# Edge aggregation on one core: dense count matrices in PSUM in place of a one-hot gather and scatter per destination tile

## The chip, the cores and the metric

The kernel runs on one core of a Trainium2 chip. The metric is the device time of one execution in microseconds (us), as the median of several runs. The core has five engines with instruction streams of their own: TensorE (PE; its weight loads are listed as PEld, its sequencer as PEq and PEldq), VectorE (DVE), ScalarE (ACT), GpSimd (POOL) and SyncE (SP), and 16 DMA engines behind queues that the engines issue to. SBUF is the on-chip memory of 128 partitions, PSUM the accumulator memory that PE writes.

## The reference

```python
N, E, D = 4096, 262144, 256
# nodes (N, D) fp32; edges_src, edges_dst (E,) int64 in [0, N); w_msg, w_self (D, D) fp32
self_out = nodes @ w_self
msg = nodes[edges_src] @ w_msg
agg = zeros((N, D)); np.add.at(agg, edges_dst, msg)
return self_out + agg
```

Each of 262,144 edges adds the transformed row of its source node to the row of its destination node. Sources and destinations are drawn at random.

## The kernel before, in words

*Keys and sort.* Each edge becomes one fp32 number that holds an integer: the tile of its destination (dst >> 7, 32 tiles of 128 nodes) in the high bits, then its source (12 bits), then dst & 127. The edges come in two halves, each with a load of 1 MB on SP's queue and on ACT's, and seven DVE instructions per half build the keys (L138 to L146). `_run_sort` sorts all 2^18 keys with a bitonic network of 18 stages. A stage is a series of DVE passes of min and max (`cpass`, L455 and around); from the eleventh stage on, each stage also transposes the 128 x 2048 array by 16 PE transposes into the layout B (L391) and 16 back (L399), whose PSUM results ACT and DVE copy out in turn. At the end the sorted keys lie as XA (rank along the free dimension) and as XB, in which a column holds 128 consecutive keys, one per partition.

*TT.* While DVE sorts, PE and ACT build TT: 256 blocks of 128 consecutive node rows in bf16, each 16 rows further than the one before, made by products with shift matrices (473 matmuls and 256 ACT copies).

*Windows.* A count over every 128th key tells for each of the 32 tiles in which column of XB its edges begin. DVE loads 31 of these numbers into a register, one by one (L190), and copies 72 columns each (L192) into a window. 18 wide passes (L202 to L210, twice) split the keys into source and destination.

*Tile loop.* For each tile, 72 chunks of 128 edges. `prep` makes the first source of each chunk, rounded down to 16, and the number of the block of TT that covers it (`bidx`, memory for PE's registers). `slabs` makes one-hot matrices for 12 chunks at a time: Sslab (128 edges x 12 chunks x 128 destinations, L261) and Eslab (the same with sources relative to the block, L268), 6 + 6 instructions on DVE per tile, the chunk being the middle dimension and the compared column the innermost. `chunkloop` runs on PE: two products Eslab^T x Sslab (L301) give a 128 x 128 count matrix of source by destination per chunk, ACT copies the pair to bf16 (L309), and a second product multiplies it with the block of TT (L316, 256 columns), adding up in agg_ps. The block's address is a register that PE's sequencer has loaded, eight at a time (`load_reg_group`, TENSOR_LOAD at L291), and turned into an address by an instruction that the order lists as ISA and the trace as FUSED_REGOPS. `tail` transposes the sum, multiplies it with w_msg and the tile's nodes with w_self, and stores 128 rows.

The Tile framework places waits by the names of tiles; within an engine the instructions run in the order of the program (a scheduler may move them, and the rows in the section on the change are in the final order).

Of the kernel before, what the change touches and what calls it, by code (L numbers as in the profile page):

```python
# [9 lines left out]
P = 128  # L10
FP32 = mybir.dt.float32
# [5 lines left out]
AX = mybir.AxisListType  # L17

CAP = 72
SLAB = 12  # L20
TT_GRAN = 16
LAG = 4
# [7 lines left out]
def kernel(  # L30
# [9 lines left out]
    nc = tc.nc  # L40
# [29 lines left out]
    iota_i = const.tile([P, P], I32, name="iota_i")  # L70
    nc.gpsimd.iota(iota_i[:], pattern=[[1, P]], base=0, channel_multiplier=0)
    iota_row = const.tile([P, P], BF16, name="iota_row")
    nc.vector.tensor_copy(out=iota_row[:], in_=iota_i[:])
    ones_col = const.tile([P, 1], FP32, name="ones_col")
    nc.vector.memset(ones_col[:], 1.0)
    e00 = const.tile([P, P], FP32, name="e00")
    nc.gpsimd.memset(e00[:], 0.0)
    nc.gpsimd.memset(e00[0:1, :], 1.0)
    shz = const.tile([P, P], BF16, name="shz")
    nc.gpsimd.memset(shz[:], 0.0)  # L80
    shA = const.tile([P, NB8, P], BF16, name="shA")
    shB = const.tile([P, NB8, P], BF16, name="shB")
    for s in range(NB8):
        nc.gpsimd.affine_select(
            out=shA[:, s, :],
            in_=shz[:],
            compare_op=ALU.not_equal,
            fill=1.0,
            base=-TT_GRAN * s,
            pattern=[[-1, P]],  # L90
            channel_multiplier=1,
        )
        nc.gpsimd.affine_select(
            out=shB[:, s, :],
            in_=shz[:],
            compare_op=ALU.not_equal,
            fill=1.0,
            base=-TT_GRAN * s + P,
            pattern=[[-1, P]],
            channel_multiplier=1,  # L100
        )

    wcat = finp.tile([P, 4, D], BF16, name="wcat")
    nc.gpsimd.dma_start(wcat[:, 0:2, :], w_self.rearrange("(k p) f -> p k f", p=P))
    nc.gpsimd.dma_start(wcat[:, 2:4, :], w_msg.rearrange("(k p) f -> p k f", p=P))

    nodes_bf_dram = dram.tile([N, D], BF16, name="nodes_bf_dram")

    wbuf0 = wp.tile([P, T, WIN], FP32, name="wbuf0")
    wbuf1 = wp.tile([P, T, WIN], FP32, name="wbuf1")  # L110
    k16 = wp.tile([P, G16], FP32, name="k16")
    Mcmp = wp.tile([P, T, G16], FP32, name="Mcmp")
    Srow = wp.tile([P, T], FP32, name="Srow")
# [8 lines left out]
    XB = [sortp.tile([P, XBW], FP32, name=f"XB{i}") for i in range(2)]  # L122

    HC = NCOL // 2
    ekey = XA[1][:].bitcast(I32)[:, 0:HC]
    etmp = XA[1][:].bitcast(I32)[:, HC:2 * HC]
    for h in range(2):
        d64 = XB[0][:, 0:NCOL].bitcast(I64)
        s64 = XB[1][:, 0:NCOL].bitcast(I64)
# [8 lines left out]
        nc.vector.tensor_single_scalar(out=ekey, in_=dlo, scalar=7, op=ALU.logical_shift_right)  # L138
        nc.vector.tensor_single_scalar(out=ekey, in_=ekey, scalar=19, op=ALU.logical_shift_left)
        nc.vector.tensor_single_scalar(out=etmp, in_=slo, scalar=7, op=ALU.logical_shift_left)  # L140
        nc.vector.tensor_tensor(out=ekey, in0=ekey, in1=etmp, op=ALU.bitwise_or)
        nc.vector.tensor_single_scalar(out=etmp, in_=dlo, scalar=127, op=ALU.bitwise_and)
        nc.vector.tensor_tensor(out=ekey, in0=ekey, in1=etmp, op=ALU.bitwise_or)
        nc.vector.tensor_copy(out=XA[0][:, h * HC:(h + 1) * HC], in_=ekey)
    for i in range(2):
        nc.gpsimd.memset(XB[i][:, NCOL:XBW], SENT_KEY)  # L146

    stgn = tc.alloc_tile_pool(name="stage_n", bufs=1)
    nodes_bf = stgn.tile([P, N // P, D], BF16, name="nodes_bf")
    nc.gpsimd.dma_start(nodes_bf[:], nodes.rearrange("(b p) f -> p b f", p=P))  # L150
    nc.sync.dma_start(nodes_bf_dram.rearrange("(b p) f -> p b f", p=P), nodes_bf[:])
    psum_tt = tc.alloc_tile_pool(name="psum_tt", bufs=1, space=bass.MemoryType.PSUM)
    for k in range(NBLK):
        j0, s = divmod(k, NB8)
        ttps = psum_tt.tile([P, D], FP32, name="tt_ps", tag="ttps", bufs=2)
        two = (s != 0) and (j0 < (N // P) - 1)
        nc.tensor.matmul(  # L157
            out=ttps[:], lhsT=shA[:, s, :], rhs=nodes_bf[:, j0, :], start=True, stop=not two
        )
        if two:  # L160
            nc.tensor.matmul(  # L161
                out=ttps[:], lhsT=shB[:, s, :], rhs=nodes_bf[:, j0 + 1, :],
                start=False, stop=True,
            )
        nc.scalar.copy(out=TT[:, k, :], in_=ttps[:])  # L165
    psum_tt.release()
    stgn.release()

    psum_sort = tc.alloc_tile_pool(name="psum_sort", bufs=1, space=bass.MemoryType.PSUM)
    _run_sort(nc, psum_sort, XA, XB, ident, NCOL, NSTAGE, JBITS, G16)  # L170

    nc.vector.tensor_copy(out=k16[:], in_=XA[0][:, 0::P])
    for t in range(T):
        nc.vector.tensor_scalar(
            out=Mcmp[:, t, :], in0=k16[:], scalar1=float(t << 19), scalar2=None, op0=ALU.is_lt
        )
    nc.vector.tensor_reduce(out=Srow[:], in_=Mcmp[:], axis=AX.X, op=ALU.add)
    c0_ps = psum_sort.tile([1, T], FP32, name="c0_ps")
    nc.tensor.matmul(out=c0_ps[:], lhsT=ones_col[:], rhs=Srow[:], start=True, stop=True)
    nc.vector.tensor_scalar(  # L180
        out=startf[:], in0=c0_ps[:], scalar1=-1.0, scalar2=0.0, op0=ALU.add, op1=ALU.max
    )
    nc.vector.tensor_copy(out=starti[:], in_=startf[:])
    psum_sort.release()

    for t in range(T):
        if t == 0:
            src_view = XB[0][:, 0:WIN]
        else:
            c0 = nc.vector.value_load(starti[0:1, t:t + 1], min_val=0, max_val=NCOL - 1)  # L190
            src_view = XB[0][:, bass.ds(c0, WIN)]
        nc.vector.tensor_copy(out=wbuf0[:, t, :], in_=src_view)  # L192

    TW = T * WIN
    HT = TW // 2
    w0f = wbuf0[:].rearrange("p t w -> p (t w)")
    w1f = wbuf1[:].rearrange("p t w -> p (t w)")
    for h in range(2):
        hs = slice(h * HT, (h + 1) * HT)
        tmp1 = XA[1][:].bitcast(I32)[:, 0:HT]  # L200
        tmp2 = XB[1][:, 0:NCOL].bitcast(I32)[:, 0:HT]
        nc.vector.tensor_copy(out=tmp1, in_=w0f[:, hs])  # L202
        nc.vector.tensor_single_scalar(out=tmp2, in_=tmp1, scalar=7, op=ALU.logical_shift_right)
        nc.vector.tensor_single_scalar(out=tmp2, in_=tmp2, scalar=4095, op=ALU.bitwise_and)
        nc.vector.tensor_copy(out=w1f[:, hs], in_=tmp2)
        nc.vector.tensor_single_scalar(out=tmp2, in_=tmp1, scalar=19, op=ALU.logical_shift_right)
        nc.vector.tensor_single_scalar(out=tmp2, in_=tmp2, scalar=7, op=ALU.logical_shift_left)
        nc.vector.tensor_single_scalar(out=tmp1, in_=tmp1, scalar=127, op=ALU.bitwise_and)
        nc.vector.tensor_tensor(out=tmp2, in0=tmp2, in1=tmp1, op=ALU.bitwise_or)
        nc.vector.tensor_copy(out=w0f[:, hs], in_=tmp2)  # L210
    sortp.release()
    wdst = wbuf0
    wsrcf = wbuf1

    psum = ctx.enter_context(tc.tile_pool(name="psum", bufs=1, space=bass.MemoryType.PSUM))
    bidxp = ctx.enter_context(tc.tile_pool(name="bidxp", bufs=1))
    bidx_all = bidxp.tile([1, T * WIN], I32, name="bidx_all")
    tp_pool = ctx.enter_context(tc.tile_pool(name="tilework", bufs=2))
    oh_pool = ctx.enter_context(tc.tile_pool(name="onehot", bufs=4))
# [271 lines left out]
```

## Time and profile before

| | us |
|---|---|
| median of 3 runs | 1254.68 (1254.49 to 1255.6) |
| span of the profiled execution | 1253.1 |
| keys | 0 to 27.2 |
| first ten sort stages, with TT built beside them | 27.2 to 166.0 |
| other sort stages, with transposes | 166.0 to 520.1 |
| windows | 520.1 to 567.6 |
| tile loop | 567.6 to 1243.8 |
| tail after the last slab | 1243.8 to 1253.1 |

The stages were cut by the times of the first and last instruction of the lines above. The page says of a span how much of it each engine was busy; a busy engine is one on which an instruction of its data path runs. Loads of registers, address arithmetic, waits and branches are not in that share, and have rows of their own under the names of the sequencers. The row of a group of instructions gives the line, engine, operation, output and inputs, their shapes and count, and after the bar the total busy time in us and the mean of one in ns, then the idle time of the engine just before them. The row of a stage gives, after its limits and length, the busy time (and count) of PE, PEld, DVE, ACT and POOL in it, then the granted clock of PE as a share of full speed, the busy share of the DMA engines and GB/s.

### The profile page before, as it was taken

To read this page: it belongs to the slowest core of one execution; us is meant where nothing else is said; L and a number is where in the kernel's file an instruction comes from. 1 tells how busy PE (TensorE), PEld (TensorE's weight loads), DVE (VectorE), ACT (ScalarE), POOL (GpSimd) and SP (SyncE) were. 2 spreads that over 40 slices of the span, in tenths; PEclk is the share of its full clock that TensorE was granted. 3 is DMA by queue.
4 is the path that set the end of the run, shared out by engine and by line. 5 is a ranking of instruction groups with operands and counts; after the bars stand their busy time and mean duration, and the time that the engine had idled before them with its cause. 6 is when DMAs were issued, how large, how long until landed. Compare 5 with 4: busy or idle time off the path is not lost.

```text
span 1253.1 us, 18139 instructions
## 1 busy us (share of the span) xinstructions
PE 674.5 (54%) x5611; PEld 500.7 (40%) x5611; DVE 1171.3 (93%) x1207; ACT 550.6 (44%) x1641; POOL 8.7 (1%) x31
## 2 busy tenths in 40 slices
PE   0777221212121121105777777777777777787777
PEld 0444110111010010004556655655665656565655
DVE  5999989899989989859999999999999999999997
ACT  0777211101010010104656565666666666665665
POOL 2000000000000000000000000000000000000000
PEclk9999665555565555557999899989899989999999
DMA  9100000000000000000000000000000000000000
GB/s 226 51 1 1 0 1 0 0 0 1 0 0 0 0 0 1 0 0 7 12 8 14 8 14 8 14 8 14 8 15 8 14 8 14 8 14 8 14 8 9
DMA packets 24279, 16.11 MB, mean 13 GB/s; under 512 B 10880, under 2 KB 23680, under 8 KB 23680
## 3 DMA queue, kind: packets, MB, share of 16 engines
q1 hardware_dynamic: 16944, 8.40, 2.3%
q0 software_dynamic: 4656, 2.36, 1.4%
q10 hardware_dynamic: 2592, 4.20, 0.9%
q8 instruction: 54, 0.88, 0.3%
q14 instruction: 33, 0.27, 0.1%
HBM read 8.91 MB, written 6.29 MB: 12 GB/s over the span
## 4 chain that ended last, share of the span: by engine, by line
DVE 90%; PE 5%; issue 2%; DMA 1%; DVEq 1%; ACT 0%; ACTq 0%
DVE Eslab L268 25%; DVE Sslab L261 25%; DVE XA_151 L430 5%; DVE XA_150 L430 5%; DVE XA_151 L431 5%; DVE XA_150 L431 5%; DVE XB_152 L430 3%; DVE XB_153 L430 3%; PE tp_sw L391 3%; DVE XB_153 L431 3%; DVE XB_152 L431 3%; DMA XB_152<-in_edges_dst_dram 1%; DVEq L190 1%; DVE base_i L228 1%; DVE wbuf_136 L192 0%
## 5 line engine op out<-in xcount | busy, mean ns | idle before, releaser
L309 ACT CAST dt_sb<-dt_ps 128x256 bf16<-128x256 f32 x1152 | 394.2, 376 | 249.9 <-PE dt_ps L301 244.4
L316 PE MATMUL agg_ps<-TT,dt_sb 128*128 x2304 | 426.7, 287 | 90.0 <-ACT dt_sb L309 68.3
L301 PE MATMUL dt_ps<-Sslab,Eslab 128*128 128x128 bf16 x2304 | 319.2, 229 | 63.1 <-DVE Eslab L268 58.0
L261 DVE TENSOR_TENSOR Sslab<-wbuf_136,iota_t 128x1536 bf16<-128x1536 f32 x192 | 336.2, 1751 | 0.0
L268 DVE TENSOR_TENSOR Eslab<-srcloc,iota_row 128x1536 bf16<-128x1536 bf16 x192 | 336.0, 1751 | 0.0
L301 PEld LDWEIGHTS <-Eslab 128*128 128x128 bf16 x2304 | 221.0, 103 | 128.8 <-DVE Eslab L268 91.4
L316 PEld LDWEIGHTS <-dt_sb 128*128 128x128 bf16 x2304 | 202.0, 102 | 130.0 <-issue 122.4
L165 ACT CAST TT<-tt_ps 128x256 bf16<-128x256 f32 x256 | 83.8, 373 | 40.7 <-PE tt_ps L161 22.4
L157 PE MATMUL tt_ps<-nodes_bf,shA 128*128 128x256 bf16 x256 | 69.9, 274 | 54.1 <-DMA nodes_bf<-in_nodes_dram 28.5
L430 DVE TENSOR_TENSOR XA_151<-XA_150 128x1024 f32<-128x1024 f32 x56 | 68.6, 1225 | 2.2
L430 DVE TENSOR_TENSOR XA_150<-XA_151 128x1024 f32<-128x1024 f32 x55 | 67.4, 1225 | 2.2
L431 DVE TENSOR_TENSOR XA_151<-XA_150 128x1024 f32<-128x1024 f32 x56 | 68.3, 1219 | 0.0
L431 DVE TENSOR_TENSOR XA_150<-XA_151 128x1024 f32<-128x1024 f32 x55 | 67.0, 1219 | 0.0
L391 PE MATMUL tp_sw<-ident,XA_150 128*128 128x128 f32 x80 | 20.0, 431 | 87.4 <-DVE XA_150 L431 68.9
L382 ACT COPY XB_152<-tp_sw 128x128 f32<-128x128 f32 x40 | 15.1, 377 | 106.0 <-PE tp_sw L391 103.4
L161 PE MATMUL tt_ps<-nodes_bf,shB 128*128 128x256 bf16 x217 | 59.9, 276 | 0.0
L391 PE MATMUL tp_sw<-ident,XA_151 128*128 128x128 f32 x64 | 15.7, 432 | 81.9 <-DVE XA_151 L431 81.9
L391 PEld LDWEIGHTS tp_sw<-ident,XA_150 128*128 128x128 f32 x80 | 14.2, 189 | 92.9 <-DVE XA_150 L431 69.8
L391 PEld LDWEIGHTS tp_sw<-ident,XA_151 128*128 128x128 f32 x64 | 11.5, 189 | 86.5 <-DVE XA_151 L431 52.6
L382 ACT COPY XB_153<-tp_sw 128x128 f32<-128x128 f32 x32 | 12.0, 377 | 73.9 <-PE tp_sw L391 71.8
L161 PEld LDWEIGHTS <-shB 128*128 128x128 bf16 x217 | 20.9, 96 | 53.7 <-issue 47.0
L157 PEld LDWEIGHTS <-shA 128*128 128x128 bf16 x256 | 25.0, 97 | 36.0 <-issue 28.4
(457 smaller groups left out, 505.8 us busy)
## 6 DMA issues: line engine op xcount, KB each, us to landing
XB_153<-in_edges_src_dram ACTq DMA_DIRECT2D x2, 1024.0 KB, 9.3
XB_152<-in_edges_dst_dram SPq DMA_DIRECT2D x2, 1024.0 KB, 8.5
nodes_bf<-in_nodes_dram POOLq DMA_DIRECT2D x1, 2048.0 KB, 20.9
nodes_bf_dram<-nodes_bf SPq DMA_DIRECT2D x1, 2048.0 KB, 8.7
out_dram<-o_sb SPq DMA_DIRECT2D x16, 128.0 KB, 1.9
out_dram<-o_sb ACTq DMA_DIRECT2D x16, 128.0 KB, 1.7
nodesT_t<-nodes_bf_dram SPq DMA_TRANSPOSE x64, 2.3
wcat<-in_w_self_dram POOLq DMA_DIRECT2D x1, 128.0 KB, 4.0
```

Source lines behind the costliest of these rows:

```text
L157: nc.tensor.matmul(out=ttps[:], lhsT=shA[:, s, :], rhs=nodes_bf[:, j0, :], start=True, stop=not two)
L161: nc.tensor.matmul(out=ttps[:], lhsT=shB[:, s, :], rhs=nodes_bf[:, j0 + 1, :], start=False, stop=True,)
L165: nc.scalar.copy(out=TT[:, k, :], in_=ttps[:])
L261: nc.vector.tensor_tensor(out=Ss[:], in0=wdst[:, t, cs].unsqueeze(2).to_broadcast([P, SLAB, P]), in1=cx["iota_t"][:].unsqueeze(1).to_broad ...
L268: nc.vector.tensor_tensor(out=Es[:], in0=cx["srcloc"][:, cs].unsqueeze(2).to_broadcast([P, SLAB, P]), in1=iota_row[:].unsqueeze(1).to_broa ...
L301: nc.tensor.matmul(out=dt2_ps[:, k, :], lhsT=E_slabs[q][:, ci, :], rhs=S_slabs[q][:, ci, :], start=True, stop=True,)
L309: nc.scalar.copy(out=dt2_sb[:], in_=dt2_ps[:])
L316: nc.tensor.matmul(out=agg_ps[:], lhsT=dt_sbs[c], rhs=TT[:, bass.ds(regs[c], 1), :].squeeze(1), start=(c == 0), stop=(c == WIN - 1),)
L382: nc.scalar.copy(out=out_ap, in_=in_ap)
L391: nc.tensor.transpose(tp[:], src[:, g * P:(g + 1) * P], ident[:])
L430: nc.vector.tensor_tensor(out=lo_d, in0=lo_s, in1=hi_s, op=ALU.min)
L431: nc.vector.tensor_tensor(out=hi_d, in0=lo_s, in1=hi_s, op=ALU.max)
```

## The change

The keys are ordered otherwise: segment of the destination (dst >> 9, eight of 512 nodes), block of the source (src >> 7, 32 blocks of 128 nodes), dst & 511, src & 127. All edges of one segment and one block are a *run*; there are 256, of about 1024 edges or eight chunks each. The sort is the same code.

The 32 node tiles are transposed by 64 DMAs on SP's queue into XT and multiplied by w_msg ahead of the sort; the result, Y, stays in SBUF in bf16. TT, its shift matrices and the windows go.

Each chunk of 128 sorted edges is taken where it lies in XB. Two one-hots, of src & 127 (128 columns) and of the place of dst in a window of 96 columns, are multiplied on PE into a 128 x 96 part of the run's 128 x 512 count matrix, which lies in one of six banks of PSUM (`ring`). The offset of the window in the ring is computed for all 2048 chunks after the sort, goes through memory (`pd`, `poffs`), and is loaded into PE's registers eight at a time. A chunk that a run begins in is multiplied a second time with a window at the run's start (`head_mm`, fixed offset, which also starts the sum in the bank); the keys of these 256 chunks are fetched by two indirect DMAs on POOL's queue. When a run is complete, ACT copies its 512 columns to bf16 (`evac`), and four products with Y (`apply_run`, 256 columns each) add it into out_ps; after 32 runs the segment's 512 rows are stored. One instruction makes the one-hots of 16 chunks, with the chunk as the innermost dimension of the tile, so that a chunk's one-hot is read by PE with a step of 16 elements.

Since a window of 96 columns and the static plan of runs (a margin of 10 chunks) need not hold for every list of edges, the kernel checks them on the chip and computes a flag. At the end each engine loads it, and a general path (`_any_edges`) runs if it is not zero.

The diff, cut to its core:

```diff
-CAP = 72
-SLAB = 12
-TT_GRAN = 16
-LAG = 4
+SEGW = 512
+W = 96
+SL = 16
+RING = 6
+MARG = 10
+LAG = 10
+NRUN = 256
...
-        nc.vector.tensor_single_scalar(out=ekey, in_=dlo, scalar=7, op=ALU.logical_shift_right)
...
-        nc.vector.tensor_copy(out=XA[0][:, h * HC:(h + 1) * HC], in_=ekey)
+        nc.vector.tensor_single_scalar(out=dhi, in_=dlo, scalar=9, op=ALU.logical_shift_right)
+        nc.vector.tensor_single_scalar(out=shi, in_=slo, scalar=7, op=ALU.logical_shift_right)
+        nc.vector.scalar_tensor_tensor(
+            out=key, in0=dlo, scalar=128.0, in1=slo, op0=ALU.mult, op1=ALU.add
+        )
+        nc.vector.scalar_tensor_tensor(
+            out=key, in0=dhi, scalar=float((1 << 21) - (1 << 16)), in1=key, ...
+        nc.vector.scalar_tensor_tensor(
+            out=key, in0=shi, scalar=float((1 << 16) - P), in1=key, ...
...
+    jrow = const.tile([P, P, SL], BF16, name="jrow")       # built on POOL
...
+            nc.sync.dma_start(                             # 64 times
+                XT[:, k, t * P:(t + 1) * P],
+                nodes_bf_dram[t * P:(t + 1) * P, k * P:(k + 1) * P], transpose=True)
+        # Y[:, t, :] = XT tile (two products) x w_msg, copied by ACT
...
     _run_sort(nc, psum_sort, XA, XB, ident, NCOL, NSTAGE, JBITS, G16)
...
+    nc.scalar.dma_start(xs_dram..., srt[:])
+    nc.vector.tensor_copy(out=k16i[:], in_=srt[:, 0::P])
+    tss(out=gi[:], in_=k16i[:], scalar=7, op=ALU.logical_shift_right)
+    # dl, ex, gb: base of each chunk's window
+    nc.sync.dma_start(gd[0, :]..., gb[:])
+    nc.sync.dma_start(gball[:], gd[0:1, :].broadcast_to([P, NCOL]))
+    # rho, rhoc, sl, wr, poff: offset of the window in the ring
+    nc.scalar.dma_start(pd[0, :]..., poff[:])
+    nc.scalar.dma_start(poffs[:], pd[0:1, :])
+    # per 512 columns: ki = dst part, kl = src & 127 (DVE), slo_b = bf16 of kl (ACT)
+    # two ACT activations (Sign, accumulated) over gball count the chunks ahead of each run
+    # cnt, cidx; two indirect DMAs on POOL fetch xh, PE transposes it, DVE makes hsl, hrel
+        tt(out=rel_b[:, s], in0=ki[:, s], in1=gball[:, s], op=ALU.subtract)
...
+    ring = psum2.tile([P, RING * SEGW], FP32, name="ring")
+    out_ps = psum2.tile([P, SEGW // P, D], FP32, name="out_ps")
...
+    def onehots(src, rel, tag):
+        e = ohp.tile([P, P, SL], BF16, name="e_oh", tag="e" + tag, bufs=8 if tag == "c" else 2)
+        tt(out=e[:], in0=src.unsqueeze(1).to_broadcast([P, P, SL]), in1=jrow[:], op=ALU.is_equal)
+        d = ohp.tile([P, W, SL], BF16, name="d_oh", tag="d" + tag, bufs=8 if tag == "c" else 2)
+        tt(out=d[:], in0=rel.unsqueeze(1).to_broadcast([P, W, SL]), in1=jrow[:, 0:W, :],
+           op=ALU.is_equal)
+        return e, d
+    def count_mm(ap, e, d, ci, start, after=()):
+        mm = nc.tensor.matmul(
+            out=ap, lhsT=e[:, :, ci], rhs=d[:, :, ci], start=start, stop=True, ...
+    def evac(r):
+        at = ohp.tile([P, SEGW], BF16, name="at", tag="at", bufs=4)
+        b = (r % RING) * SEGW
+        ins = nc.scalar.copy(out=at[:], in_=ring[:, b:b + SEGW]).ins
...
+    def head_mm(r, he, hd_):
+        count_mm(ring[:, b:b + W], he, hd_, r % SL, True, after)
+    def apply_run(r):
...                                    # once per segment: 8 products XT x w_self into out_ps
+        for t in range(SEGW // P):
+            nc.tensor.matmul(
+                out=out_ps[:, t, :], lhsT=at[:, t * P:(t + 1) * P], rhs=Y[:, b, :],
+                start=False, stop=(b == T - 1), skip_group_check=True)
...                                    # last run of a segment: 2 ACT copies, 2 stores on SP
+        for c in range(NCOL):          # in an order written out by hand
+            # c % 16 == 0: onehots of the next 16 chunks; of 16 heads when one falls due
+            # head_mm of the run that begins 8 * r - MARG
+            if c % 8 == 0:
+                nc.tensor.load(regs, poffs[0:1, c:c + 8])
+            off = nc.tensor.snap(regs[c % 8], ...)
+            count_mm(ring[:, bass.ds(off, W)], e, d, ci, False)
+            # evac of a run MARG chunks after its nominal end, apply_run LAG chunks later
...
+    # check: small DVE instructions and four DMAs through kd and fd make the flag
+    cond = nc.values_load(flag[0:1, 0:1], min_val=0, max_val=1 << 16)
+    with tc.If(cond > 0):
+        _any_edges(tc, edges_src, edges_dst, out, XT, Y, wcat, ident, N, D, E, T)
```

The lines of the changed kernel that the prediction names: the one-hots are L301 and L303, the count products L316, evac L332, the products with Y L358, the load of offsets L389.

PE's order in the loop before, where a tile's second products begin among its first ones; dt_sb is the count matrix in bf16, agg_ps the sum:

```order
L301 LDWEIGHTS Eslab
L301 MATMUL dt_ps<-Sslab,Eslab 128x128
L316 LDWEIGHTS dt_sb
L291 TENSOR_LOAD bidx_all
L316 ISA
L316 MATMUL agg_ps<-TT,dt_sb 128x256
L316 LDWEIGHTS dt_sb
L316 ISA
L316 MATMUL agg_ps<-TT,dt_sb 128x256
```

Of two products per chunk, the second has a register in the address of what it reads (TT); the load of eight registers stands between a weight load and its product.

PE's order in the loop after, around a head product (the pair without ISA) and the next load of offsets; the number behind a name is that of the buffer:

```order
L316 LDWEIGHTS e_oh_2161
L316 MATMUL ring_1608<-d_oh_2163,e_oh_2161 128x96
L316 LDWEIGHTS e_oh_2197
L316 ISA
L316 MATMUL ring_1608<-d_oh_2199,e_oh_2197 128x96
L316 LDWEIGHTS e_oh_2197
L316 ISA
L316 MATMUL ring_1608<-d_oh_2199,e_oh_2197 128x96
L316 LDWEIGHTS e_oh_2233
L389 TENSOR_LOAD poffs_1533
L316 ISA
L316 MATMUL ring_1608<-d_oh_2235,e_oh_2233 128x96
```

One product per chunk is left, and the register has moved to the address of what it writes (ring). The load still comes once in eight chunks.

DVE's order between sort and loop before, at the last window (L190 loads the register, L192 copies) and the first of two groups of wide passes:

```order
L190 TENSOR_LOAD starti
L190 ISA x2
L192 ISA
L192 COPY wbuf_136<-XB_152 128x72
L202 CAST XA_151<-wbuf_136 128x1152
L203 TENSOR_SCALAR XB_153<-XA_151 128x1152
L204 TENSOR_SCALAR XB_153<-XB_153 128x1152
L205 CAST wbuf_137<-XB_153 128x1152
```

DVE's order after, from the end of the check to the first one-hots; xt_ps is the transposed result of the indirect DMAs:

```order
L435 TENSOR_REDUCE bcol<-bad 128x1
L261 TENSOR_SCALAR cnt<-cnt 128x2
L264 TENSOR_SCALAR cidx<-cnt 128x2
L279 CAST hs_i<-xt_ps 128x128 x2
L280 TENSOR_SCALAR hd_i<-hs_i 128x256
L281 TENSOR_SCALAR hs_i<-hs_i 128x256
L283 TENSOR_TENSOR hrel<-hd_i,hbase 128x256
L282 CAST hsl<-hs_i 128x256
L438 TENSOR_REDUCE bsum<-brow 1x1
L301 TENSOR_TENSOR e_oh<-hsl,jrow 128x2048
L303 TENSOR_TENSOR d_oh<-hrel,jrow 128x1536
L301 TENSOR_TENSOR e_oh<-slo_b,jrow 128x2048
```

The register loads and window copies on DVE are gone, and in their place DVE waits for the heads' keys (L279) ahead of the loop's first one-hots.

More of the change, by code (lines that the diff above doesn't have):

```diff
@@ L68 @@
+    pd = dram.tile([1, NCOL], I32, name="pd")
+    fd = dram.tile([1, P], FP32, name="fd")
+    rd = dram.tile([1, NCOL + 64], I32, name="rd")
     ident = const.tile([P, P], FP32, name="ident")
     make_identity(nc, ident[:])
[L70 to L101, printed above, removed]
@@ L153 @@
[L153 to L165, printed above, removed]
@@ L178 @@
[L178 to L192, printed above, removed]
@@ L211 @@
[L211 to L219, printed above, removed]
-    dt_pool = ctx.enter_context(tc.tile_pool(name="dtsb", bufs=LAG + 2))
-    out_v = out.rearrange("(t p) f -> t p f", p=P)
@@ L252, in prep @@
             )
-        return dict(srcloc=srcloc, bidx=bidx, iota_t=iota_t, nodesT_t=nodesT_t)
-    def slabs(t, cx):
-        S_slabs = []
-        E_slabs = []
-        for q in range(NSLAB):
-            cs = slice(q * SLAB, (q + 1) * SLAB)
-            Ss = oh_pool.tile([P, SLAB, P], BF16, name="Sslab", tag="Sslab")
+    psum_y = tc.alloc_tile_pool(name="psum_y", bufs=1, space=bass.MemoryType.PSUM)
+    for t in range(T):
+        y_ps = psum_y.tile([P, D], FP32, name="y_ps", tag="y_ps", bufs=2)
+        for k in range(2):
+            nc.tensor.matmul(
+                out=y_ps[:], lhsT=XT[:, k, t * P:(t + 1) * P], rhs=wcat[:, 2 + k, :],
+                start=(k == 0), stop=(k == 1),
+            )
+        nc.scalar.copy(out=Y[:, t, :], in_=y_ps[:])
@@ new lines @@
+    nc.vector.tensor_scalar(
+        out=cnt[:], in0=cnt[:], scalar1=0.5, scalar2=float(NCOL // 2 - 1), op0=ALU.mult, op1=ALU.add
+    )
+    nc.vector.tensor_scalar(
+        out=cidx[:], in0=cnt[:], scalar1=0.0, scalar2=None, op0=ALU.max
+    )
+    hs_i = meta.tile([P, NRUN], I32, name="hs_i")
+    hd_i = meta.tile([P, NRUN], I32, name="hd_i")
+    hsl = meta.tile([P, NRUN], BF16, name="hsl")
+    hrel = meta.tile([P, NRUN], BF16, name="hrel")
+    for h in range(2):
+        xh = meta.tile([P, P], FP32, name=f"xh{h}")
+        nc.gpsimd.indirect_dma_start(
+            out=xh[:], out_offset=None, in_=xs_dram[:, :],
+            in_offset=bass.IndirectOffsetOnAxis(ap=cidx[:, h:h + 1], axis=0),
+        )
+        xt_ps = psum_sort.tile([P, P], FP32, name="xt_ps", tag="tp", bufs=4)
+        nc.tensor.transpose(xt_ps[:], xh[:], ident[:])
+        nc.vector.tensor_copy(out=hs_i[:, h * P:(h + 1) * P], in_=xt_ps[:])
@@ L356 @@
-    cxs = [prep(0)]
-    slabs(0, cxs[0])
-    for t in range(T):
-        if t + 1 < T:
-            cxs.append(prep(t + 1))
-        chunkloop(t, cxs[t])
-        tail(t, cxs[t])
-        if t + 1 < T:
-            slabs(t + 1, cxs[t + 1])
+                out=sel[:], in0=df[:].to_broadcast([P, P]), in1=dt[:], op=ALU.is_equal
+            )
+            s_ps = ps.tile([P, D], FP32, name="g_s_ps")
+            nc.tensor.matmul(out=s_ps[:], lhsT=sel[:], rhs=g[:], start=True, stop=True)
+            nc.vector.tensor_tensor(out=o[:], in0=o[:], in1=s_ps[:], op=ALU.add)
```

480 lines of the change are left out of this document (304 added, 176 removed).

## The prediction

> **What bounds the kernel now.** I read the page's busy shares and chain first, then the busy times by stage, then the costliest groups, and last the rows of PE's sequencer, which no busy share counts.
>
> ```profile
> span 1253.1 us, 18139 instructions
> PE 674.5 (54%) x5611; PEld 500.7 (40%) x5611; DVE 1171.3 (93%) x1207; ACT 550.6 (44%) x1641; POOL 8.7 (1%) x31
> DVE 90%; PE 5%; issue 2%; DMA 1%; DVEq 1%; ACT 0%; ACTq 0%
> L261 DVE TENSOR_TENSOR Sslab<-wbuf_136,iota_t 128x1536 bf16<-128x1536 f32 x192 | 336.2, 1751 | 0.0
> L268 DVE TENSOR_TENSOR Eslab<-srcloc,iota_row 128x1536 bf16<-128x1536 bf16 x192 | 336.0, 1751 | 0.0
> ```
>
> The chain is DVE for 90% of the span, and over half of DVE is the 384 one-hot slabs. By stage (time; busy PE, PEld, DVE, ACT, POOL; granted clock; DMA share, GB/s):
>
> ```profile
> 27.20:166.00 138.80, 82.03 (x473) 45.73 (x472) 136.60 (x120) 83.80 (x256) 0.00 (x0) 0.89 0.06 16
> 166.00:520.10 354.10, 64.12 (x256) 46.44 (x256) 323.80 (x370) 41.04 (x128) 0.00 (x0) 0.55 0.00 0
> 520.10:567.60 47.50, 5.33 (x21) 3.68 (x22) 27.10 (x100) 3.01 (x8) 0.00 (x0) 0.50 0.00 0
> 567.60:1243.80 676.20, 518.41 (x4824) 401.70 (x4824) 672.07 (x605) 418.12 (x1239) 0.00 (x0) 0.93 0.04 11
> 1243.80:1253.10 9.30, 4.62 (x38) 3.06 (x38) 0.00 (x0) 3.37 (x10) 0.00 (x0) 0.96 0.05 16
> ```
>
> Keys take 27.2 us, the sort 492.9, the windows 47.5, the tile loop 676.2 with DVE never idle, the tail 9.3. The span lies 1.6 us under the runs' median of 1254.68, and I add 1.6 to every span below.
>
> **The change, part by part.** *Keys.* Per half, seven DVE instructions become five.
>
> ```profile
> 13.02 8.66 DMA XB_152<-in_edges_dst_dram
> 21.78 0.69 DVE L138 TENSOR_SCALAR XA_151<-XB_152 128x1024 int32<-128x1024 int32 x1 [0.50 <-DMA XB_152<-in_edges_dst_dram]
> 23.23 1.23 DVE L141 TENSOR_TENSOR XA_151<-XA_151 128x1024 int32<-128x1024 int32 x1
> 27.21 0.69 DVE L418 TENSOR_SCALAR XA_150<-XA_150 128x1024 f32<-128x1024 f32 x1
> ```
>
> A fused multiply-add of two tensors isn't in the trace; between 0.69 and 1.23 us I take 1.23, as it reads two tensors. The second loads wait for the last reader of the first (0.69+0.69+1.23 after the first landing, about 11.7 instead of 13.0), land near 20.4, and 0.69x2+1.23x3 plus two small ones end near 25.8 instead of 27.2: -1.4 (-3 to +3, as POOL's wide constants now run beside it). The sort itself, 492.9 us, is the same code. The new Y products and 64 transposed loads go ahead of the sort's first transposes on PE, which come at 166 us:
>
> ```profile
> nodesT_t<-nodes_bf_dram SPq DMA_TRANSPOSE x64, 2.3
> out_dram<-o_sb SPq DMA_DIRECT2D x16, 128.0 KB, 1.9
> wcat<-in_w_self_dram POOLq DMA_DIRECT2D x1, 128.0 KB, 4.0
> XB_152<-in_edges_dst_dram SPq DMA_DIRECT2D x2, 1024.0 KB, 8.5
> 567.11 7.54 SPq L248 DMA_TRANSPOSE nodesT_t<-nodes_bf_dram  x6
> ...
> 166.37 4.00 PE tp_sw L391 x16
> ```
>
> SP issues six in 7.54 us, so 64 take about 80 us and are done near 125; the sort up to 166 is DVE's alone, which hides them, and the 32 ACT copies that replace 256. Without that cover they would delay the sort's eleventh stage one for one. Removed for nothing on the path: the shift matrices and TT (473 matmuls of the second stage).
>
> *Between sort and first matmul.* Out go 31 register loads on DVE (0.78 us apart) and 18 wide passes; before, PE's first slab product comes 54.7 us after the sort:
>
> ```profile
> 528.89 0.20 DVE L192 COPY wbuf_136<-XB_152 128x72 f32 x1 [0.58 <-issue]
> 529.66 0.20 DVE L192 COPY wbuf_136<-XB_152 128x72 f32 x1 [0.57 <-issue]
> 574.79 1.25 PE L301 MATMUL dt_ps<-Sslab,Eslab 128*128 128x128 bf16 x10 [3.70 <-DVE Eslab L268]
> ...
> L228 DVE TENSOR_SCALAR base_i<-base_i 128x72 int32<-128x72 int32 x32 | 6.3, 198 | 1.0
> ```
>
> In comes a chain, since PE's first head product needs hsl and hrel: nine small DVE instructions to gb (0.2 each like L228: 1.8), gb to memory (2), the 1 MB broadcast gball (8.5), four rel_b of 512 (0.7 each, at 1.02 ns an element as below: 2.8), the first e_oh and d_oh, which stand ahead (2.0), ten check instructions and cnt, cidx (2.4), POOL's two gathers (4.0+1), transposes, casts and four 256-wide passes (2.1), the head one-hots (2.0): 29 us. kd, pd, fd, poffs and the four 512-wide groups of ki and kl lie under gball's transfer. DVE is queued behind gball and behind the gathers, PE behind DVE. With gball at half its price 22, with transfers half again as long 40. So the loop begins at 518.7+29 = 547.7.
>
> *One-hots.* 128 chunk slabs and 16 head slabs, each e_oh (2048 wide) and d_oh (1536). Now the chunk is innermost, both inputs are 16-bit and step by one. No row shows that. The bounds are one element a cycle, as in Eslab (1751 ns for 1536 and L141's 1230 for 1024, so 1.02 ns an element and 2.28 us for 2048), and two a cycle, as here:
>
> ```profile
> 518.89 1.23 DVE L455 COPY XA_150<-XA_151 128x2048 f32<-128x2048 f32 x1
> 571.40 1.67 DVE Sslab L261
> 573.07 5.00 DVE Eslab L268 x3
> ```
>
> 2048 at two a cycle is 1.23 us, 1536 is 0.96; started back to back each costs 0.08 less, as 1.751 does in steps of 1.67. A pair is 2.02 us (3.87 at one a cycle), 144 pairs 291 us (557). I take two a cycle: Eslab is the nearest operation, but in its innermost dimension one input stands still, and the edit changes just that; L455, whose input and output both step by one, has the pace. [...]
>
> *PE's sequencer.* Here the gain ends. Each chunk's product writes at an offset in a register, and each eight offsets are loaded by PE's sequencer. Before, agg_ps has the same pattern (2304 and 288 times; now 2048 and 256):
>
> ```profile
> L291 PEldq TENSOR_LOAD <-bidx_all x288: 587/591/853, 576.1 to 1246.1; - x144
> L316 PEldq FUSED_REGOPS  x2304: 46/46/46, 577.0 to 1247.8; - x192
> L291 PEldq TENSOR_LOAD <-bidx_all x3: 591/591/592, 580.3 to 583.7; - x3
> 930.67 1.14 PE L316 MATMUL agg_ps<-TT,dt_sb 128*128 x8 [0.19 <-issue]
> ```
>
> A load blocks the sequencer for 591 ns. The last eight products of a tile run one per (1.14-0.27)/7 = 124 ns (0.27 is one's duration), though 256 columns need 109 (below): the sequencer sets their pace. Three loads in a row, with nothing else to hold them, start at 580.3 and 583.7: 1.70 us for eight chunks = 0.591 + 8x0.124 + 0.11. Before, 288x1.70 = 490 us lay under DVE's 676. Now DVE needs 291, and 256x1.70 = 435 is the longest. One term shrinks: the address takes two register operations instead of three, so 31 to 46 ns; eight times that bounds the period by 1.58 and 1.70. I take 1.66, since a fixed part of the 46 must remain: 425 us (404 to 435).
>
> *PE's array* must stay under 1.66. Per eight chunks it has eight count products and one head product of 96 columns and four at x Y of 256.
>
> ```profile
> 911.48 0.61 PE L301 MATMUL dt_ps<-Sslab,Eslab 128*128 128x128 bf16 x8
> 908.43 0.38 PE L316 MATMUL agg_ps<-TT,dt_sb 128*128 x2
> 908.65 0.27 PE L301 MATMUL dt_ps<-Sslab,Eslab 128*128 128x128 bf16 x2
> 908.76 0.38 PE L316 MATMUL agg_ps<-TT,dt_sb 128*128 x2
> 396.25 0.19 PEld L399 LDWEIGHTS tp_sw_1990<-ident,XB_153 128*128 128x128 f32 x1
> ...
> L391 PEld LDWEIGHTS tp_sw<-ident,XA_150 128*128 128x128 f32 x80 | 14.2, 189 | 92.9 <-DVE XA_150 L431 69.8
> L309 ACT CAST dt_sb<-dt_ps 128x256 bf16<-128x256 f32 x1152 | 394.2, 376 | 249.9 <-PE dt_ps L301 244.4
> ...
> 395.30:398.60 3.30, 3.21 (x15) 0.50 0.00 0
> ```
>
> Eight products of 128 columns take 0.61 and two 0.27, so each further one 56 ns; a group of two and two takes 0.33 (908.43 to 908.76), so 256 columns take 109. 9x0.056+4x0.109 = 0.94 us, 57% of 1.66; the second stage held a clock of 0.89 with 473 such matmuls (37%). But e_oh and d_oh are read in steps of 32 bytes. Weights read in steps of 64 bytes (L399) took 0.19 as contiguous ones did (L391), at clock 0.50. Unhidden, the price lies between 56 ns and the 0.22 of a whole fp32 transpose there (3.30/15); I take 56 to 109, either of which hides. [...]
>
> *Evacuation and tail.* ACT has two 512-wide casts per 3.3 us, under 0.6 each (L309's 256 take 0.376), hidden. After the last chunk: two casts, eight products, two copies, the store: 6 us. The check's answer needs no work: the widest chunk of the drawn edges needs 96 of the 96 columns and none fails, so the general path is only branched over, 1.5 us (0 to 5), which no row shows.
>
> *Sum.* 518.7 + 29 + 425 + 6 + 1.5 = 980.2, and 1.6: about 982 us.
>
> **Rivals.** *DVE alone binds*, if a register offset on the output is far cheaper than 124 ns and the load overlaps: 518.7+29+142x2.02+3+7.5+1.6 = 847. The rows of the load speak against it. 0.05.
> *PE's array binds through strided reads.* From (1.66-0.44)/9 = 136 ns per count product on; at 160 the period is 1.88 and the time about 1038, at 200 2.24 and 1130. Against it stands the equal 0.19. [...] 0.10.
> *One-hots at one a cycle*: 518.7+29+142x3.87+3+7.5+1.6 = about 1109. For it, Eslab is 16-bit and has it. 0.04.
> *Slower than before:* strided products take the fp32 transpose's 0.22 and the clock stays at half, where 256 columns take 0.213: 9x0.22+4x0.213 = 2.83 per period, 725 us, 1282 in all. It decides from 0.21 each at that clock. It needs both; the clock was 0.93 in the loop. 0.03.
>
> **How the numbers follow.** The sequencer's bound has 0.78 and runs from 945 (22 us of chain, 404) to 1010 (40, 435), further with the unknowns of DMA and branch. Left out of 940 to 1060 are the first rival, the third, the fourth, half of the second and the edges of the forecast: 0.20. All cases but the last are faster by over 0.2%, about the least a measurement of this kernel can tell: 0.96, with 0.01 for no change and 0.03 for slower.
>
> **What would show it.** Right: TENSOR_LOAD rows of poffs 1.6 to 1.7 us apart through the loop; PE idle on "issue"; DVE's slabs at 1.23 and 0.96 us but waiting for PE, busy about 70% of the loop; the first ring product some 29 us after the sort. Wrong: count products over 136 ns apart without issue gaps, a loop near 290 us, slabs of 2.28 us, or a chain of transfers much over 40 us.

## The result and the profile after

The changed kernel took 1194.77 us (median of 4 runs, 1193.75 to 1195.58) against 1254.59 before: ratio 0.9523, 95% interval 0.9509 to 0.9536. The forecast was 982 us, with a range of 940 to 1060: the sign was right, the size was not. The profiled execution has a span of 1193.3 us.

From the page: span, busy shares, the granted clock in 40 slices, the chain, and the three costliest groups of the loop.

```profile
span 1193.3 us, 11711 instructions
PE 731.0 (61%) x3730; PEld 554.1 (46%) x3730; DVE 786.4 (66%) x851; ACT 222.2 (19%) x449; POOL 18.1 (2%) x24
PEclk9999995555565555555555555565555555655555
...
PE 58%; DVE 37%; DMA 3%; issue 1%; ACT 0%; DVEq 0%; SPq 0%
...
L316 PE MATMUL ring<-d_oh,e_oh 128*128 128x96 bf16 x2304 | 460.7, 361 | 5.4 <-DVE d_oh L303 5.0
L301 DVE TENSOR_TENSOR e_oh<-slo_b,jrow 128x2048 bf16<-128x2048 bf16 x128 | 156.7, 1224 | 302.6 <-PE ring L316 302.6
L303 DVE TENSOR_TENSOR d_oh<-rel_b,jrow 128x1536 bf16<-128x1536 bf16 x128 | 121.6, 950 | 0.0
```

The chain, 90% DVE before, is now 58% PE and 1% issue: TensorE's data path binds the loop, not its sequencer. DVE's slabs cost what was forecast and then wait 302.6 us for PE. The clock stays near half through the whole loop, where it was 0.93 before.

By stage (columns as in the prediction): keys, sort, the way to the first ring product, loop, tail. The cut at 26.50 lies 1.5 us before the end of the keys; the sort's first instruction starts at 28.06.

```profile
0.00:26.50 26.50, 0.00 (x0) 0.00 (x0) 11.05 (x11) 1.28 (x1) 16.03 (x22) 1.00 0.78 207
26.50:520.59 494.09, 89.38 (x320) 53.23 (x320) 461.54 (x492) 52.85 (x160) 0.00 (x0) 0.67 0.05 11
520.59:550.57 29.98, 5.39 (x18) 3.13 (x19) 19.04 (x65) 9.38 (x16) 2.07 (x2) 0.50 0.25 77
550.57:1184.40 633.83, 633.39 (x3381) 496.25 (x3382) 294.73 (x285) 156.49 (x268) 0.00 (x0) 0.52 0.02 7
1184.40:1193.30 8.90, 2.80 (x14) 1.45 (x11) 0.00 (x0) 2.15 (x4) 0.00 (x0) 0.69 0.18 62
```

Windows and tile loop together took 723.7 us before; the way to the loop and the loop take 663.8 now. Outside the loop the forecast holds to within 2 us: the sort ends at 520.59 instead of 518.7, the way to the loop takes 29.98 instead of 29, the tail 8.90 instead of 7.5. The loop, forecast at 425, took 633.8.

One period of it on PE (start, length, count), and the registers' loads:

```profile
591.14 1.82 PE L316 MATMUL ring<-d_oh,e_oh 128*128 128x96 bf16 x9
592.77 1.03 PE L358 MATMUL out_ps<-Y,at 128*128 128x256 bf16 x4
593.60 1.79 PE L316 MATMUL ring<-d_oh,e_oh 128*128 128x96 bf16 x9
...
L389 PEldq TENSOR_LOAD <-poffs x256: 587/590/1317, 550.6 to 1179.2; - x128
```

A row's length runs to the modelled end of its last product, so the pace is read from the starts: nine count products fill the 1.63 us from 591.14 to 592.77, 181 ns each (179 at the median of the loop's groups of nine), and four products with Y the 0.83 us to 593.60. The period is 2.46 us where 1.66 was forecast, and 256 x 2.46 = 630. The loads cost the forecast 590 ns, but lie under the products.

### The profile page after: what moved, and what is told of

Its sections match the earlier page's. It is cut to its first block, busy times and chain, and to the rows that moved or that the text cites. A ratio compares the mean times of both kernels' runs of the same rounds, so it can differ in the third digit from the quotient of the medians.

```text
span 1193.3 us, 11711 instructions
## 1 busy us (share of the span) xinstructions
PE 731.0 (61%) x3730; PEld 554.1 (46%) x3730; DVE 786.4 (66%) x851; ACT 222.2 (19%) x449; POOL 18.1 (2%) x24
## 4 chain that ended last, share of the span: by engine, by line
PE 58%; DVE 37%; DMA 3%; issue 1%; ACT 0%; DVEq 0%; SPq 0%
PE ring L316 34%; PE out_ps L358 18%; DVE XA_85 L567 6%; DVE XA_84 L567 6%; DVE XA_85 L568 5%; DVE XA_84 L568 5%; DVE XB_86 L567 3%; DVE XB_87 L567 3%; DVE XB_87 L568 3%; DVE XB_86 L568 3%; PE tp_sw L528 3%; DMA XB_86<-in_edges_dst_dram 1%; PE out_ps L353 1%; DMA fd<-bcol 1%; DMA kd<-k_1518 0%
## 5 line engine op out<-in xcount | busy, mean ns | idle before, releaser
L316 PE MATMUL ring<-d_oh,e_oh 128*128 128x96 bf16 x2304 | 460.7, 361 | 5.4 <-DVE d_oh L303 5.0
L316 PEld LDWEIGHTS <-e_oh 128*128 128x128 bf16 x2304 | 348.3, 151 | 87.2 <-issue 6.1
L301 DVE TENSOR_TENSOR e_oh<-slo_b,jrow 128x2048 bf16<-128x2048 bf16 x128 | 156.7, 1224 | 302.6 <-PE ring L316 302.6
L358 PE MATMUL out_ps<-Y,at 128*128 128x256 bf16 x1024 | 259.2, 407 | 0.0
L332 ACT CAST at<-ring 128x512 bf16<-128x512 f32 x256 | 150.0, 586 | 488.6 <-PE ring L316 488.6
L358 PEld LDWEIGHTS <-at 128*128 128x128 bf16 x1024 | 140.1, 137 | 52.9 <-ACT at L332 0.4
L303 DVE TENSOR_TENSOR d_oh<-rel_b,jrow 128x1536 bf16<-128x1536 bf16 x128 | 121.6, 950 | 0.0
L182 PE MATMUL y_ps<-wcat,XT 128*128 128x256 bf16 x64 | 25.2, 394 | 100.0 <-DMA XT<-nodes_bf_dram 100.0
L567 DVE TENSOR_TENSOR XA_85<-XA_84 128x1024 f32<-128x1024 f32 x56 | 68.6, 1225 | 2.2
L567 DVE TENSOR_TENSOR XA_84<-XA_85 128x1024 f32<-128x1024 f32 x55 | 67.4, 1225 | 2.2
L568 DVE TENSOR_TENSOR XA_85<-XA_84 128x1024 f32<-128x1024 f32 x56 | 68.2, 1218 | 0.0
L568 DVE TENSOR_TENSOR XA_84<-XA_85 128x1024 f32<-128x1024 f32 x55 | 67.0, 1218 | 0.0
L567 DVE TENSOR_TENSOR XB_86<-XB_87 128x1024 f32<-128x1024 f32 x30 | 36.7, 1225 | 1.0
L567 DVE TENSOR_TENSOR XB_87<-XB_86 128x1024 f32<-128x1024 f32 x30 | 36.7, 1225 | 1.0
L519 ACT COPY XB_86<-tp_sw 128x128 f32<-128x128 f32 x40 | 14.9, 376 | 119.2 <-PE tp_sw L528 116.9
L568 DVE TENSOR_TENSOR XB_87<-XB_86 128x1024 f32<-128x1024 f32 x30 | 36.5, 1218 | 0.0
L568 DVE TENSOR_TENSOR XB_86<-XB_87 128x1024 f32<-128x1024 f32 x30 | 36.5, 1217 | 0.0
```

What stands on the lines that cost most here:

```text
L182: nc.tensor.matmul(out=y_ps[:], lhsT=XT[:, k, t * P:(t + 1) * P], rhs=wcat[:, 2 + k, :], start=(k == 0), stop=(k == 1),)
L301: tt(out=e[:], in0=src.unsqueeze(1).to_broadcast([P, P, SL]), in1=jrow[:], op=ALU.is_equal)
L303: tt(out=d[:], in0=rel.unsqueeze(1).to_broadcast([P, W, SL]), in1=jrow[:, 0:W, :], op=ALU.is_equal,)
L316: mm = nc.tensor.matmul(out=ap, lhsT=e[:, :, ci], rhs=d[:, :, ci], start=start, stop=True, skip_group_check=True,).ins
L332: ins = nc.scalar.copy(out=at[:], in_=ring[:, b:b + SEGW]).ins
L358: nc.tensor.matmul(out=out_ps[:, t, :], lhsT=at[:, t * P:(t + 1) * P], rhs=Y[:, b, :], start=False, stop=(b == T - 1), skip_group_check=True,)
```

## The experiments

A product has two operands, and the trace lists them in two rows: a LDWEIGHTS on PEld that reads e_oh (2304 of them at L316), and a MATMUL on PE that names d_oh ahead of e_oh. Below, e_oh is called the weights and d_oh the moving operand. Three theories were set against the 179 ns: the step of the moving operand, d_oh (A), the step of the weights, e_oh (B), and the sequencer (C).

**d_oh read contiguously.**

```diff
-            out=ap, lhsT=e[:, :, ci], rhs=d[:, :, ci], ...
+            rhs=d[:].rearrange("p a b -> p (a b)")[:, ci * W:(ci + 1) * W]
```

> The count product reads 96 contiguous columns of d_oh (the values are those of other chunks), e_oh is still read in steps of 32 bytes. Three theories on the 179 ns per count product of the changed kernel (9 in 1.61 us). A, the moving operand: reading d_oh in steps of 32 bytes takes twice the time; then the product falls to what the weight load leaves, 107 to 125 ns, the period of eight chunks from 2.47 to 1.81-1.98 us, and the time to 1025-1070 us. B, the weights: loading e_oh in steps of 32 bytes takes 179 ns; then nothing changes, 1190-1200 us. C, the sequencer (a register offset on the output): nothing changes either.

991.62 us, ratio to before 0.7899 (0.7876 to 0.7922). One edit of one operand takes away 203 us. Its loop, two loads of registers in a row, and PE in one period:

```profile
552.00:980.00 428.00, 338.61 (x3364) 307.98 (x3363) 291.70 (x284) 155.18 (x267) 0.00 (x0) 0.99 0.03 10
...
700.52 0.46 PE L316 MATMUL ring<-d_oh,e_oh 128*128 128x96 bf16 x5
701.31 0.59 PE L316 MATMUL ring<-d_oh,e_oh 128*128 128x96 bf16 x4 [0.34 <-issue]
701.74 0.60 PE L358 MATMUL out_ps<-Y,at 128*128 128x256 bf16 x4
702.18 0.47 PE L316 MATMUL ring<-d_oh,e_oh 128*128 128x96 bf16 x5
702.97 0.62 PE L316 MATMUL ring<-d_oh,e_oh 128*128 128x96 bf16 x4 [0.32 <-issue]
```

Here is the loop that the prediction described: from 701.31 to 702.97 one period of 1.66 us (1.63 in other places), PE idle on issue once in it while the sequencer loads eight registers, and the clock at 0.99. C falls here already, and so does B, which had no change. A had the right operand but too high a time, 1025 to 1070 us: the clock rose, and the price of a product is not the 107 to 125 ns that A left for it, since five in a row (702.18) start some 65 ns apart (0.47 us less the 0.21 of the last, over four).

**e_oh read contiguously**, d_oh in steps (the same edit on lhsT).

> The mirror image: the weights e_oh are read contiguously (values of other chunks), d_oh in steps of 32 bytes. A: no change, 1190-1200 us. B: the product falls to the 80 ns of 96 columns at half clock or to 107, and the time to 985-1030 us. C: no change. If both operands bind alike, either run alone gains little, and only the run with both contiguous falls.

1178.93 us: while d_oh is stepped, the weights' step is worth 16 us, where A had no change. **Both contiguous:**

> Both operands contiguous (values of other chunks); register offsets and all instructions stay. A and B: the period falls to 1.66 us (the sequencer's, as the prediction had it) if the clock rises, or 9 x 0.107 + 0.85 = 1.81 us at half clock: 985-1025 us. C: 1190-1200 us. A fourth, D, the half clock itself makes the 179 ns (128 weight columns and 96 moving ones in series, 224 columns at 1.25 a ns): no change, 1190-1200 us unless the clock rises.

992.89 us, as with d_oh alone. A holds, B falls; the clock rose here too, so this run leaves D open. The weights' step has a price all the same, which this loop hides under the sequencer. The weight loads with d_oh alone contiguous, then those with both, and five products in a row with both:

```profile
L316 PEld LDWEIGHTS <-e_oh 128*128 128x128 bf16 x2304 | 225.4, 152 | 116.6 <-issue 112.7
...
L316 PEld LDWEIGHTS <-e_oh 128*128 128x128 bf16 x2304 | 168.1, 98 | 161.4 <-issue 144.6
...
702.82 0.38 PE L316 MATMUL ring<-d_oh,e_oh 128*128 128x96 bf16 x5
```

A stepped load is recorded at 152 ns, a contiguous one at 98, and five products take 0.47 us with the first and 0.38 with the second, so they start some 65 and 44 ns apart.

**Constant offsets.**

```diff
-            if c % 8 == 0:
-                ... nc.tensor.load(regs, poffs[0:1, c:c + 8])
-            count_mm(ring[:, bass.ds(off, W)], e, d, ci, False)
+            off = (c // 8) % RING * SEGW + min(c % 8 * 60, SEGW - W)
+            count_mm(ring[:, off:off + W], e, d, ci, False)
```

> The changed kernel with both operands in steps, but with constant offsets in the ring instead of the registers (the columns of a run are then not those of its edges): 256 register loads and 2048 address instructions are gone from TensorE's sequencer. A, B and D: no change, 1185-1200 us. C: the period falls below 1.9 us and the time below 1050 us.

1191.65 us, 3 us less than the changed kernel: C falls while d_oh is stepped.

**The size of the step.** The chunk stays innermost, but in groups of G, here 8, 4 and 2, so that a chunk's one-hot is read in steps of 16, 8 and 4 bytes; nothing of the work is left out.

```diff
-    e[P, P, SL], d[P, W, SL]; lhsT=e[:, :, ci], rhs=d[:, :, ci]
+    e[P, SL // G, P, G], d[P, SL // G, W, G]; lhsT=e[:, ci // G, :, ci % G], rhs=d[:, ci // G, :, ci % G]
```

> The changed kernel with the chunk innermost in groups of 8 instead of 16: the one-hot of a chunk is read in steps of 16 bytes. After the four runs before (contiguous d_oh 991.6 us, contiguous e_oh 1178.9, both 992.9, constant offsets 1191.7) the moving operand's step sets the 179 ns. [...] Distance: if the price grows with the step, about half of the excess over contiguous goes: 1080-1100 us. VectorE: its instructions keep 1.22 and 0.95 us if runs of 8 in the innermost dimension suffice for two elements a cycle; at one a cycle VectorE alone gives 1109 us.

> [...] Distance: a quarter of the excess stays, but the sequencer's 1.63 us hides it if the clock rises: 990-1040 us. VectorE at one element a cycle would give 1109 us or more.

> Groups of 2: steps of 4 bytes. [...]

1183.11, 991.66 (ratio 0.7896, 0.7883 to 0.7909) and 989.54 us. For groups of 8 the groups of the count product and of the e_oh slabs, and one period on PE; for 4 and 2 the two groups:

```profile
L323 PE MATMUL ring<-d_oh,e_oh 128*128 128x96 bf16 x2304 | 454.6, 357 | 5.8 <-DVE d_oh L304 5.3 <-issue 0.5
L304 DVE TENSOR_TENSOR e_oh<-slo_b,jrow 128x2048 bf16<-128x2048 bf16 x128 | 156.6, 1223 | 291.2 <-PE ring L323 291.2
...
701.82 1.77 PE L323 MATMUL ring<-d_oh,e_oh 128*128 128x96 bf16 x9
703.41 1.03 PE L365 MATMUL out_ps<-Y,at 128*128 128x256 bf16 x4
```

```profile
L323 PE MATMUL ring<-d_oh,e_oh 128*128 128x96 bf16 x2304 | 311.3, 258 | 47.6 <-issue 23.3 <-DVE d_oh L304 5.4 <-DVE e_oh L304 1.2
L304 DVE TENSOR_TENSOR e_oh<-slo_b,jrow 128x2048 bf16<-128x2048 bf16 x128 | 156.4, 1222 | 115.1 <-PE ring L323 115.1
```

```profile
L323 PE MATMUL ring<-d_oh,e_oh 128*128 128x96 bf16 x2304 | 242.2, 206 | 115.2 <-issue 104.0 <-DVE d_oh L304 5.9 <-DVE e_oh L304 4.7
L304 DVE TENSOR_TENSOR e_oh<-slo_b,jrow 128x2048 bf16<-128x2048 bf16 x128 | 156.4, 1222 | 113.8 <-PE ring L323 113.8
```

The mean length of a product falls from 357 to 258 and 206 ns, and the starts of products that nothing else held lie 177, 91 and 43 ns apart (steps of 16, 8 and 4 bytes; 179 at 32). The first is nine products in 1.59 us (701.82 to 703.41); the other two are single starts, which the rows join (at 8 bytes three products fill the 0.29 us from 699.98 to 700.27, 97 each up to the first product with Y; at 4 bytes five take 0.38 from 701.19, the last of them 0.21). So a step of 16 bytes costs what one of 32 does, and below 16 the price falls about in half with each halving of the step. The 43 ns are near the 41 that 96 contiguous columns would take, by an estimate from the 109 of 256 before (a clock of 1.00). The theory of distance falls: 16 bytes are nearly as bad as 32 (1183.11 us, where distance had 1080 to 1100). Why 16 and 32 bytes cost the same was not taken apart. Both operands change their step in these runs, but e_oh alone in steps of 32 bytes gave 65 ns, so the 177 and 91 are d_oh's in the main. For groups of 4 the 91 ns don't show in the time, because the sequencer's 1.63 us hides them: 9 x 0.091 + 0.44 = 1.26 us. The groups of 4 and of 2 multiply the right values and are as fast as the contiguous reads, so it is not the values of other chunks that made those fast. DVE kept 1.22 us for 2048 elements down to runs of two, so the layout that DVE needs and the one that PE needs don't exclude each other.

**Both contiguous, constant offsets.**

> Both operands contiguous (values of other chunks) and constant offsets, so neither the step nor the sequencer can bind. The prediction's first rival then holds: VectorE's one-hots, 2.02 us a pair, 142 pairs = 287 us of loop instead of 428, 840-860 us. If TensorE's array binds instead: 9 x 0.056 + 0.44 = 0.94 us at full clock (241 us, hidden by VectorE) or 9 x 0.107 + 0.85 = 1.81 us at half clock (464 us, 1025 us).

847.45 us. In a stretch of its loop DVE is never idle:

```profile
552.00:830.00 278.00, 230.43 (x3282) 207.89 (x3281) 278.00 (x278) 151.35 (x262) 0.00 (x0) 0.98 0.05 15
```

So behind the step comes the sequencer (992.89 to 847.45, 145 us), and behind that DVE, at the 847 that the prediction had for its first rival.

**More offsets a load**, on the groups of 2.

```diff
-            if c % 8 == 0: ... 8 registers, nc.tensor.load(regs, poffs[0:1, c:c + 8])
+            if c % 16 == 0: ... 16 registers, nc.tensor.load(regs, poffs[0:1, c:c + 16])   # then 32
```

> Groups of 2 (989.5 us, TensorE's sequencer at 1.63 us a period: one load of eight registers blocks it for 0.59) with 16 offsets a load, 128 loads instead of 256. If the 0.59 us is a price per load: (0.59 + 0.12 + 16 x 0.115)/2 = 1.28 us a period, 327 us of loop instead of 428, 885-895 us. If it is a price per register: 985-995 us.

> Groups of 2 with 32 offsets a load. Price per load: 0.18 + 8 x 0.115 = 1.10 us a period, 281 us, now less than the 287 us of VectorE's one-hots, so VectorE begins to bind as with constant offsets (847 us): 850-870 us. Price per register: 985-995 us. This is the version that should beat both kernels with the reference's output.

973.65 us (0.7755, 0.7739 to 0.777) and 987.23 us (0.7859, 0.7846 to 0.7872). Their loads:

```profile
L396 PEldq TENSOR_LOAD <-poffs x128: 1101/1104/1881, 547.9 to 960.6; - x128
```

```profile
L396 PEldq TENSOR_LOAD <-poffs x64: 2127/2131/2862, 548.1 to 971.8; - x64
```

590, 1104 and 2131 ns for 8, 16 and 32 registers are 64 ns a register and some 77 fixed. The price is nearly all per register, yet neither expectation for 16 was right: 128 loads fewer save 128 x 0.077 = 10 us of the fixed part, and the time fell by 16; the other 6 were not taken apart. Why 32 registers lose 14 of them again was not taken apart; the granted clock between 552 and 940 us is 0.89 with them and 0.99 with 16. The version with 16 offsets a load is the fastest of those that leave nothing of the work out, 221 us below the changed kernel.

**The clock: every second chunk contiguous.**

```diff
+            rhs=(contiguous columns if ci % 2 else d[:, :, ci])
```

> The changed kernel, but every second chunk reads d_oh contiguously (values of other chunks), the others in steps of 32 bytes. It tells the clock apart: in the changed kernel the granted clock was 0.52 in the loop, and the four products with Y of a run took 0.85 us instead of 0.44. With 4.5 stepped products at 0.179 a period: at full clock 0.81 + 4.5 x 0.061 + 0.44 = 1.52 us of array, the sequencer's 1.63 binds, 990-1000 us. At half clock 0.81 + 4.5 x 0.107 + 0.85 = 2.14, 1110-1120 us. If the clock stays half whenever stepped reads are there, the second; if it depends on how long the array idles, the first or a value between.

993.53 us at a clock of 0.99:

```profile
552.00:980.00 428.00, 415.36 (x3347) 372.91 (x3347) 292.07 (x284) 154.52 (x266) 0.00 (x0) 0.99 0.03 10
```

**And each product with Y twice**, all chunks stepped.

> The changed kernel (steps of 32 bytes) with each product with Y issued twice (its part of the result doubles): 1024 more contiguous products of 256 columns. It tells what held the clock at half. If stepped reads hold it there as such: 9 x 0.179 + 8 x 0.213 = 3.32 us a period, 850 us of loop, 1405-1420 us. If it is the share of time in which columns go into the array (at half clock 9 x 80 + 853 ns of 2.47 us, 64%, in the changed kernel; 78% in the run with every second chunk contiguous, whose clock was 0.99), here it would be (720 + 1706) of 3.32 us, 73%: if that is enough, 9 x 0.165 to 0.179 + 8 x 0.109 = 2.36 to 2.48 us, 1165-1200 us, the time of the changed kernel with 1024 products more; if the threshold lies above 73%, as in the first case.

1204.98 us: 1024 products more cost 10 us (5 above the range given for a clock that rises, and far from the 1405 to 1420 for one that stays at half). The loop's row and one period:

```profile
552.00:1190.00 638.00, 638.00 (x4358) 537.47 (x4357) 292.92 (x283) 155.35 (x266) 0.00 (x0) 0.99 0.02 7
...
699.22 1.05 PE L358 MATMUL out_ps<-Y,at 128*128 128x256 bf16 x8
700.11 1.79 PE L316 MATMUL ring<-d_oh,e_oh 128*128 128x96 bf16 x9
701.72 1.06 PE L358 MATMUL out_ps<-Y,at 128*128 128x256 bf16 x8
```

At full clock nine stepped products still take 1.61 us (700.11 to 701.72), so their price does not hang on the clock, and D falls; eight products with Y take 0.89 us, where four took 0.83 at half clock. Stepped reads as such do not hold the clock down (0.99 with every chunk stepped). What does was not isolated. The shares that the expectation estimates from the products' times, 64% in the changed kernel (clock 0.52) and 78% and 73% in these two (0.99), stand in the order of the clocks; that the clock follows them was not shown.

At full clock the changed kernel's period would be 1.61 + 0.44 = 2.05 us, by estimate. So of the 203 us that a contiguous d_oh takes away, about half (256 x 0.41 = 105 us) came by way of the clock; the rest came directly, down to the 1.63 to 1.66 us at which the sequencer binds.

## Why the prediction was wrong, point by point

*Keys and sort.* Forecast to end at 518.7, ended at 520.59. The keys ended at 28.0 instead of 25.8, and the sort took 492.5 us of the forecast 492.9. The fused key instructions took the 1.22 us assumed. The first of all (L105) took 3.23 us instead of the 0.69 that it takes in the second half, with POOL busy for 16 of the first 25 us; this overlap the range had named, and no run took it apart. Y was hidden as said: the last of its products starts at 124.8, against an estimate of 125.

*The chain to the loop.* 29 forecast, 29.98 measured, with errors that cancel: the 1 MB broadcast took 4.6 us instead of 8.5, the two gathers 6.7 (538.19 to 544.89) instead of 5, and check and rel_b were placed otherwise. That the sum came out close is partly luck.

*One-hots.* 1.224 and 0.950 us for the forecast 1.23 and 0.96: the pace of L455, 2048 elements in 1.23 us, and the third rival is out.

*Sequencer.* 1.66 us a period forecast, 1.63 to 1.66 measured, in the run with contiguous d_oh, where nothing hides it. That run takes 991.62 us, 10 more than the 982 forecast. The term was right; it was not the largest.

*The array: the step that failed.* "Weights read in steps of 64 bytes (L399) took 0.19 as contiguous ones did (L391)", and from it the price of a count product was taken as 56 to 109 ns. That row shows a weight load. Count products read the other operand, the moving one, in steps too, and no row of before shows that; the run with e_oh contiguous and the one with d_oh contiguous show how unlike the two are. Nor did the row carry over to the weights: it is an fp32 load, and the bf16 loads of e_oh are recorded at 152 ns stepped and 98 contiguous. The term measures 179 ns, beyond the 136 from which the prediction said the array would bind. So its second rival came true, the one given 0.10, by the sign that it had named, count products over 136 ns apart without issue gaps.

*The clock.* The rival was priced at full clock, and half clock only beside a price of 0.22. With 0.179 and half clock together its own formula gives 9 x 0.179 + 4 x 0.213 = 2.46 us (before, at a clock of 0.50, two products of 128 columns and two of 256 took 0.64 us, 904.46 to 905.10, so 256 columns 0.213), 630 for the loop and 518.7 + 29 + 630 + 7.5 + 1.6 = 1187, 8 us from the result. The reason given against half clock, 0.93 in the loop before, did not carry over. Nor does the clock go by the profile's busy time: here PE was busy for 633.39 of the loop's 633.83 us and was granted 0.52, and with d_oh contiguous it was busy for 338.61 of 428 and was granted 0.99.

*Tail and branch.* 7.5 forecast, 8.9 measured. No run shows the 1.5 us of the branch by itself: the last product ends at 1187.20, and the span 6.1 us later, with the copies, the stores and the branch in between.

*The range.* The two bounds named for the sequencer, 945 and 1010, do not follow from their terms: 518.7 + 22 + 404 + 7.5 + 1.6 is 954, and with 40 and 435 it is 1003. Neither changes the outcome.

## What to carry to other kernels

When a layout is turned round to suit VectorE, price the reads of the other engine from a row of the same operand and type: here a stepped fp32 weight load said nothing of a stepped bf16 moving operand. Where no row shows it, the price of each unknown end has to be carried through to the time with the clock that goes with it, since the clock can change with the edit (0.52 with d_oh in steps, 0.99 with it contiguous). A group as small as the writing engine's pace allows can serve both sides (here two elements: DVE kept 1.222 us, and the products started 43 ns apart).

## What the runs showed of the hardware that was not expected

- A moving operand of 96 bf16 columns costs 179 ns in steps of 32 bytes, at half clock (0.52) and at full (0.99) alike, 177 at 16, 91 at 8 and 43 at 4.
- The weights pay less for the same step: with d_oh contiguous, products start some 65 ns apart with e_oh in steps of 32 bytes and 44 without. The kernel shows nothing of it where the sequencer sets the pace (991.62 and 992.89 us), and 16 us where d_oh is stepped as well (1194.77 and 1178.93).
- A load of registers on TensorE's sequencer costs 64 ns a register and some 77 fixed (590, 1104 and 2131 ns for 8, 16 and 32).
- PE was busy for 633.39 of 633.83 us and was granted 0.52 of its clock over them; with 1024 products more it was granted 0.99, and the kernel took 10 us longer.
